# A branch prefetch hint on TensorE ahead of each expert's conditional blocks in the first expert stage

## The chip, the core and the metric

The kernel runs on one core of one Trainium2 chip. The metric is device time in microseconds (us) of one execution, lower is better. Time before: 1584.59 us, the median of 3 runs (1584.36 to 1587.86).

## The reference

Two layers of a diffusion trunk with 256 latent and 256 context tokens of width 1024. Each layer mixes the tokens (conv, pooling, two kinds of attention) and then sends them through a mixture of 16 experts, two experts for each token. Only the mixture matters here:

```python
def expert_block(args):
    xblk, e = args
    a = xblk @ w_gate[e]
    u = xblk @ w_up[e]
    return (jax.nn.silu(a) * u) @ w_down[e]

yb = lax.map(expert_block, (xb, block_exp)).reshape(n_blocks * MOE_BLOCK, d)
y_assign = yb[dest] * sw[:, None].astype(h.dtype)
return jax.ops.segment_sum(y_assign, st, num_segments=t_tok)
```

In the first layer all 512 tokens go through it, so 1024 rows are spread over 16 experts, 64 on average. How many an expert gets is known only when the router has run.

## The kernel before

**The first expert stage** is `moe0`. Experts are taken in order, `e` from 0 to 15. The rows of an expert are cut into chunks of 32. Chunks 0 and 1 are always computed (`gu(e, [0, 1], ...)`: gate and up products, 128 matmuls on TensorE, then `swiglu` on ScalarE and VectorE). A third chunk is computed under `tc.If(v > 64)` and a fourth under `tc.If(v > 96)`, where `v = counts[e]` is the number of rows; inside that, under `tc.If(v > 128)`, there are two loops for still more rows. Each of these extra chunks ends with its own down product (`down_x`, line 1085, 64 matmuls). After the conditional blocks `down(e)` computes the down product of chunks 0 and 1 (line 1076, 32 matmuls) and a scatter on GpSimd writes the rows to `yd` in device memory.

**Control flow.** Each engine has its own instruction stream and its own copy of the conditions in registers. A condition is a COMPARE_AND_BRANCH on each engine; the body of the `If` lies straight behind it and is jumped over when the condition does not hold. The code that is jumped over on TensorE is long: for `v > 64` two gate and up products, two loops with their bodies and two down products; for `v > 96` the same less one of each; for `v > 128` only the two loops. The conditions have the lines 1146, 1148 and 1151 in the profile of before. Line 1127 is a small condition inside `fetch_more`, in which TensorE has no work of its own.

**Order.** The stage stands under `tc.manual_schedule()`, so that each engine takes its instructions in the order in which they are written. For TensorE that is, for one expert: chunks 0 and 1 (line 1023), branch on 64, branch on 96 where it is reached, the extra down products, then `down(e)`, then the next expert.

**Weights.** `Ring` loads 12 pieces of 1 MB for each expert (four pairs of gate and up, four of down) into 11 units of on-chip memory of two pieces each, from the SP queue (`big_load`, line 178), with at most four loads in flight. A load waits until TensorE has read the old content of its place. Ahead of the stage the ring is filled.

**After the stage** the loads of `yd` (line 1180) on the SP queue wait for the last scatter, and loads of `w_mod` for the second layer (line 178) stand behind them on the same queue. The matmuls of line 213 use those.

The lines that the change touches, with their callers:

## Time and profile before

| what | value |
|---|---|
| median of 3 runs | 1584.59 us (1584.36 to 1587.86) |
| the profiled execution, its own time | 1585.9 us |
| its span, first to last instruction | 1584.4 us |
| TensorE matmul busy | 1339.8 us, 85% of the span |
| VectorE busy | 507.2 us, 32% |
| ScalarE busy | 244.5 us, 15% |
| mean rate of all transfers | 324 GB/s |
| waits of TensorE's line 1076 on its own queue at line 1146 | 29.5 us in 8 |
| waits of TensorE's line 1085 on its own queue at line 1148 | 7.6 us in 2 |

Busy shares are means over the whole program. The first expert stage runs from 357.7 to 877.2 us. An engine's queue (PEq or PEldq for TensorE, DVEq for VectorE, SPq for SP) is its sequencer: the branches, waits and transfers that it handles itself are not counted as busy. "PE <- PEq L1146" means that the matmul unit had nothing to do until TensorE's own sequencer was through with the branch of line 1146.

### The profile page before, as it was taken

The numbers are of one execution on the slowest core, as the hardware profiler recorded it, in microseconds if no ns is written. First come the engines' busy times: TensorE is split into PE (matmuls) and PEld (weight loads), VectorE is DVE, ScalarE is ACT, GpSimd is POOL, SyncE is SP. The second block draws the span as 40 slices with busy tenths as digits, with TensorE's granted clock in tenths as the row PEclk, the third lists the DMA queues.
The fourth block names the chain that finished last, engine by engine and source line by source line (L and its number), as shares of the span: only waits on it lengthen the run. The fifth ranks groups of instructions, "written<-read, shape, count | busy, mean of one in ns | idle before, by whom it ended". The sixth has DMA issues, their size and how long they took to land. (4 is left out here: it accounts for less than half of the span.)

```text
span 1584.4 us, 22716 instructions
## 1 busy us (share of the span) xinstructions
PE 1339.8 (85%) x9054; PEld 576.5 (36%) x9054; DVE 507.2 (32%) x1350; ACT 244.5 (15%) x536; POOL 188.0 (12%) x254
## 2 busy tenths in 40 slices
PE   4999999859889887888898299996888898988987
PEld 1754555433222222222332067642332232323333
DVE  2555365671111101111112568743212112112121
ACT  3432143110000000000001265410000000000000
POOL 0411200231111110011110431110000000000000
PEclk9999989979889898999999699997999999999999
DMA  9677875267999999999986753665998899999991
GB/s 362 207 276 266 284 276 200 80 242 279 419 420 420 418 416 419 417 418 418 407 333 195 292 196 121 239 251 212 420 419 356 323 416 419 419 414 420 410 415 40
DMA packets 92349, 513.11 MB, mean 324 GB/s; under 512 B 15872, under 2 KB 19328, under 8 KB 36320
## 3 DMA queue, kind: packets, MB, share of 16 engines
q1 hardware_dynamic: 84320, 490.47, 77.7%
q0 software_dynamic: 6096, 18.42, 3.1%
q8 instruction: 138, 2.26, 0.6%
q10 hardware_dynamic: 1712, 1.27, 0.3%
q14 instruction: 83, 0.68, 0.1%
HBM read 501.80 MB, written 8.32 MB: 322 GB/s over the span
## 5 line engine op out<-in xcount | busy, mean ns | idle before, releaser
L1023 PE MATMUL psg<-u,W 128*32 128x512 f32 x4608 | 531.5, 612 | 68.2 <-DMA u<-in_w_up_dram 15.0
L1023 PEld LDWEIGHTS psg<-u,W 128*32 128x32 f32 x4608 | 159.0, 112 | 428.1 <-issue 364.5
L1076 PE MATMUL pd<-u,W 128*64 128x512 f32 x512 | 135.6, 683 | 39.2 <-PEq L1146 29.5
L1030 DVE TENSOR_TENSOR W<-W,psg 128x256 f32<-128x256 f32 x72 | 30.3, 421 | 381.2 <-ACT W L1029 339.9
L1061 DVE STREAM_TRANSPOSE W<-W 128x256 f32<-128x256 f32 x49 | 30.0, 635 | 324.6 <-DMA W<-h2d,W 297.3
L1232 PE MATMUL pd<-u,x 128*64 128x512 f32 x544 | 120.5, 594 | 15.3 <-DVE x L1031 10.4
L1029 ACT ACTIVATE W<-psg 128x256 f32<-128x256 f32 x72 | 27.6, 383 | 586.8 <-PE psg L1023 567.0
L1076 PEld LDWEIGHTS pd<-u,W 128*64 128x64 f32 x512 | 43.1, 156 | 129.3 <-issue 119.9
L756 PE MATMUL ps<-u,u 128*128 128x512 f32 x192 | 90.1, 614 | 0.0
L213 PE MATMUL psm<-u,W 128*32 128x512 f32 x320 | 47.2, 669 | 35.1 <-DMA u<-in_w_mod_dram 21.7
L1232 PEld LDWEIGHTS pd<-u,x 128*64 128x64 f32 x544 | 44.9, 137 | 84.2 <-issue 78.9
L1053 POOL DMA_INDIRECT W<-h2d,W x49 | 46.9, 956 | 153.5 <-DVE W L1061 132.1
L1057 POOL DMA_INDIRECT yd<-W x23 | 22.9, 996 | 284.0 <-ACT W L1064 261.1
L328 DVE TENSOR_TENSOR x<-u,x 128x512 fp32r<-128x512 f32 (+2 forms) x64 | 42.0, 660 | 42.0 <-ACT x L327 37.6
L1085 PE MATMUL pd<-u,W 128*32 128x256 f32 x448 | 35.5, 462 | 22.5 <-PEq L1148 7.6
L756 PEld LDWEIGHTS ps<-u,u 128*128 128x128 f32 x192 | 35.6, 195 | 43.2 <-issue 42.9
L327 ACT CAST x<-u 128x512 fp32r<-128x512 f32 (+2 forms) x64 | 35.4, 562 | 98.2 <-PE ps L402 46.8
L1234 DVE SCALAR_TENSOR_TENSOR W<-pd,W,x 128x512 f32<-128x512 f32 x17 | 12.8, 751 | 111.2 <-PE pd L1232 111.2
L403 PE MATMUL ps<-u,x 128*128 128x512 f32 (+1 forms) x128 | 44.9, 351 | 1.1 <-DVE x L328 1.0
L401 PE MATMUL ps<-u,x 128*128 128x512 f32 (+1 forms) x128 | 45.2, 353 | 0.0
L1064 ACT COPY W<-pd 128x512 f32<-128x512 f32 (+1 forms) x23 | 12.0, 520 | 212.8 <-PE pd L1076 154.0
L402 PE MATMUL ps<-u,x 128*128 128x512 f32 (+1 forms) x128 | 44.3, 346 | 0.0
(283 smaller groups left out, 1459.7 us busy)
## 6 DMA issues: line engine op xcount, KB each, us to landing
u<-in_w_gate_dram SPq DMA_DIRECT2D x128, 1024.0 KB
u<-in_w_up_dram SPq DMA_DIRECT2D x128, 1024.0 KB
u<-in_w_down_dram SPq DMA_DIRECT2D x128, 1024.0 KB
u<-in_w_mod_dram SPq DMA_DIRECT2D x40, 1024.0 KB
u<-in_w_in_dram SPq DMA_DIRECT2D x12, 1024.0 KB
x<-in_w_mod_dram SPq DMA_DIRECT2D x8, 1024.0 KB
u<-in_w_out_dram SPq DMA_DIRECT2D x4, 2048.0 KB
u<-m_dram POOLq DMA_DIRECT2D x9, 512.0 KB, 7.2
```

Source lines behind the costliest of these rows:

```text
L213: PE.matmul(ps[32 * g:32 * g + 32, :], sc[:, j, :], t[:, 512 * g:512 * g + 512], start=(j == 0), stop=(j == 7), tile_position=(0, 32 * g))
L327: i = S.copy(h, src)
L328: eng.tensor_tensor(l, src, h.bitcast(F32), op=ALU.subtract)
L401: PE.matmul(ps, xh, yh, start=first, stop=False)
L402: PE.matmul(ps, xh, yl, start=False, stop=False)
L403: PE.matmul(ps, xl, yh, start=False, stop=end)
L756: PE.matmul(ps, CT[:, k, 128 * i:128 * i + 128], wout[hh][:, k, :], start=(k == 0), stop=(k == 7))
L1023: PE.matmul(pss[k][32 * g:32 * g + 32, :], xTs[k][:, j, :], w[:, :, 256 * g:256 * g + 256], start=(j == 0), stop=(j == 7), tile_position=( ...
L1053: G.indirect_dma_start(out=XG[b], out_offset=None, in_=src, in_offset=bass.IndirectOffsetOnAxis(ap=ic, axis=0))
L1076: PE.matmul(pd[64 * h:64 * h + 64, :], HP[:, j, :], w[:, 512 * h:512 * h + 512], start=(j == 0), stop=(j == 7), tile_position=(0, 64 * h))
L1085: PE.matmul(pd[32 * g:32 * g + 32, 0:256], hT[:, j, :], w[:, 256 * g:256 * g + 256], start=(j == 0), stop=(j == 7), tile_position=(0, 32 * g))
L1232: PE.matmul(pd[64 * h:64 * h + 64, :], HT[k][:, j, :], w[:, 512 * h:512 * h + 512], start=(j == 0), stop=(j == 7), tile_position=(0, 64 * h))
```

## The change

At the start of each expert's code a hint names the branch on `v > 64`, and at the start of that branch's body a hint names the branch on `v > 96`. Each hint carries the condition's value in a register, computed by an added register operation. Both are on TensorE only. Two labels tie the hints to their branches.

```diff
                 v = counts[e]
                 if e + 1 < NE:
                     fetch(e + 1)
+                tc.mark_branch_hint_location(f"more{e}", v > 64, engines=[ET.PE])
                 gu(e, [0, 1], [0, 1], [None, None])
-                with tc.If(v > 64):
+                with tc.If(v > 64, label=f"more{e}"):
+                    tc.mark_branch_hint_location(f"most{e}", v > 96, engines=[ET.PE])
                     gu(e, [2], [2], ["o"])
-                    with tc.If(v > 96):
+                    with tc.If(v > 96, label=f"most{e}"):
                         tr(XT[0], XG[3])
                         gu(e, [0], [3], ["mod"])
                         with tc.If(v > 128):
```

In the built program TensorE has 32 register operations and 32 hints more (2 of each for each expert) and the other engines have the same instructions as before. Line numbers behind the change are higher by 1 or 2.

The next fence shows TensorE's stream at the branch on 64 of one expert. Names: `psg` is the accumulator of gate and up, `W` holds the rows, `u_...` are ring units; 1146 became 1147 and 1148 became 1150.

```order
-L1146 COMPARE_AND_BRANCH
+L1147 COMPARE_AND_BRANCH
+L1148 REGISTER_ALU
+L1380 BRANCH_PREFETCH_HINT
 L1023 MATMUL psg<-u_71,W 32x512 x8
 L1023 MATMUL psg<-u_6_1290,W 32x512 x8
 L1023 MATMUL psg<-u_64,W 32x512 x8
 L1023 MATMUL psg<-u_70,W 32x512 x8
-L1148 COMPARE_AND_BRANCH
+L1150 COMPARE_AND_BRANCH
```

The hint for the branch on 96 stands at the start of the body, one chunk's product (64 matmuls in the trace) ahead of its branch.

The next two fences show TensorE's stream from the end of the block on 64 of expert 0 to the start of expert 1, before and after (`pd` is the accumulator of the down product).

```order
L1146 UNCONDITIONAL_BRANCH x2
L1076 MATMUL pd<-u_69,W 64x512 x8
L1076 MATMUL pd<-u_67,W 64x512 x8
L1023 MATMUL psg<-u_5_1289,W 32x512 x5
L1127 COMPARE_AND_BRANCH
L1127 UNCONDITIONAL_BRANCH x2
```

After:

```order
L1147 UNCONDITIONAL_BRANCH x2
L1145 REGISTER_ALU
L1380 BRANCH_PREFETCH_HINT
L1076 MATMUL pd<-u_69,W 64x512 x8
L1076 MATMUL pd<-u_67,W 64x512 x8
L1023 MATMUL psg<-u_5_1289,W 32x512 x5
L1127 COMPARE_AND_BRANCH
L1127 UNCONDITIONAL_BRANCH x2
```

The hint for expert 1 stands ahead of `down(0)`, not behind it, so a whole down product, the small branch of line 1127 and the product of chunks 0 and 1 lie between the hint and its branch.

## Rows read from the trace of the kernel before

**Rows 1.** TensorE in order of time, experts 0 and 1 (start, length, idle before).

```profile
375.12 7.09 PE L1076 MATMUL pd<-u,W 128*64 128x512 f32 x32 [1.67 <-DVEq L1146]
382.14 13.94 PE L1023 MATMUL psg<-u,W 128*32 128x512 f32 x128
399.68 9.95 PE L1076 MATMUL pd<-u,W 128*64 128x512 f32 x32 [3.60 <-PEq L1146]
```

**Rows 2.** Four stretches: busy time of each engine, granted TensorE clock, transfer share, GB/s.

```profile
370.00:375.00 5.00, 3.45 (x35) 1.36 (x24) 2.11 (x4) 0.77 (x2) 0.00 (x0) 1.00 0.02 3
400.00:405.00 5.00, 5.00 (x14) 1.50 (x12) 0.60 (x2) 0.00 (x0) 1.89 (x2) 0.50 1.02 417
790.00:795.00 5.00, 4.31 (x27) 1.14 (x31) 0.63 (x2) 0.00 (x0) 0.00 (x0) 0.66 0.40 169
795.00:800.00 5.00, 4.46 (x44) 1.16 (x36) 0.06 (x1) 0.38 (x1) 0.00 (x0) 1.00 0.01 3
```

**Rows 3.** TensorE's queue at lines 1146, 1148, 1151, 1127: min/median/max ns, first and last start.

```profile
L1146 PEldq COMPARE_BRANCH  x22: 70/306/6524, 370.6 to 860.3; - x22
...
L1148 PEldq COMPARE_BRANCH  x7: 65/5923/6127, 454.9 to 833.3; - x7
...
L1151 PEldq COMPARE_BRANCH  x1: 329/329/329, 796.7 to 796.7; - x1
...
L1127 PEldq COMPARE_BRANCH  x17: 82/229/330, 357.7 to 846.4; - x17
```

**Rows 4.** TensorE's queue at line 1146 in expert 0 (368 to 376 us).

```profile
L1146 PEldq COMPARE_BRANCH  x1: 3843/3843/3843, 370.6 to 370.6; - x1
L1146 PEldq EVENT_SEMAPHORE  x1: 51/51/51, 374.5 to 374.5; - x1
```

**Rows 5.** TensorE's queue at line 1148 in expert 10 (660 to 680 us).

```profile
L1148 PEldq COMPARE_BRANCH  x1: 6037/6037/6037, 672.5 to 672.5; - x1
```

**Rows 6.** TensorE in order of time, experts 10 to 15 and the start of the next layer.

```profile
663.03 12.22 PE L1023 MATMUL psg<-u,W 128*32 128x512 f32 x112 [0.50 <-DMA u<-in_w_up_dram]
679.00 4.67 PE L1085 MATMUL pd<-u,W 128*32 128x256 f32 x56 [3.75 <-PEq L1148]
684.53 0.64 PE L1085 MATMUL pd<-u,W 128*32 128x256 f32 x8 [0.87 <-issue]
...
716.59 5.08 PE L1085 MATMUL pd<-u,W 128*32 128x256 f32 x64 [3.66 <-DMA u<-in_w_gate_dram]
...
753.23 4.04 PE L1085 MATMUL pd<-u,W 128*32 128x256 f32 x37 [3.81 <-PEq L1148]
758.88 1.92 PE L1085 MATMUL pd<-u,W 128*32 128x256 f32 x27 [1.60 <-issue]
...
790.69 8.77 PE L1023 MATMUL psg<-u,W 128*32 128x512 f32 x64 [2.14 <-DVE W L1061]
...
837.89 4.23 PE L1085 MATMUL pd<-u,W 128*32 128x256 f32 x64 [1.89 <-DVEq L1148]
...
867.11 10.05 PE L1076 MATMUL pd<-u,W 128*64 128x512 f32 x32 [4.11 <-PEq L1146]
...
897.11 1.94 PE L213 MATMUL psm<-u,W 128*32 128x512 f32 x8 [16.06 <-DMA u<-in_w_mod_dram]
```

**Rows 7.** The SP queue in order of time: weight loads, and the transfers behind the stage.

```profile
375.50 1.57 SPq L178 DMA_DIRECT2D u<-in_w_gate_dram  x1
...
651.26 0.33 SPq L178 DMA_DIRECT2D u<-in_w_up_dram  x1
...
881.75 2.01 SPq L1180 DMA_DIRECT2D u<-yd  x4
883.87 0.94 SPq L178 DMA_DIRECT2D u<-in_w_mod_dram  x2
```

**Rows 8.** What the SP queue waited for: us in total, times, longest.

```profile
SPq L178 <- PEq L1146: 15.9, 1, 15.9
...
SPq L1180 <- DMA yd<-W: 10.4, 1, 10.4
```

## Prediction

> **What bounds the kernel now.** I read the list of TensorE's waits first, then TensorE in order of time over the first expert stage, its own queue at the branches, the transfer share by stretches, and last the SP queue. The question is in which part of the stage TensorE sets the time and in which the weights do.

> Every expert with at most 64 rows jumps over the block of line 1146, and those with 65 to 96 rows jump over the block of line 1148. The jump is slow on TensorE's queue: up to 6.52 us at line 1146, 5.92 us in the median at line 1148, while a condition that falls through costs 0.07 us and the short jumps of lines 1127 and 1151 cost about 0.23 and 0.33 us [rows 3]. Nothing in these rows waits for data in that time, so I read it as the fetch of the instructions at the far end of the jump. In expert 0, with transfers nearly idle (share 0.02, [rows 2]), it took 3.84 us [rows 4]; in expert 10, beside the weights, 6.04 us [rows 5].

> What TensorE loses is less than that, because its queue runs ahead of its matmuls. Expert 10's product ends at 663.03 + 12.22 = 675.25 us and the branch began at 672.5 us. The next matmul comes 3.75 us after the product's end [rows 5, 6]. Some wait would stay with a free branch: the down product needs the activation and the transpose on ScalarE and VectorE. Where the branch is not last this is 1.67 us (expert 0, [rows 1]) and 1.89 us (expert 14, [rows 6]).

> Two further costs hang on the slow jump. First, the granted clock: after expert 1's wait of 3.60 us the clock was 0.50 in 400 to 405 us, the lower level, and `down` took 9.95 us where expert 0's took 7.09 us [rows 1, 2]. Second, the block of instructions behind the target: expert 10 stops again after 56 of 64 matmuls, until 684.53 us, that is 6.0 us after the branch ended at 672.5 + 6.04 = 678.54 us [rows 5, 6]; expert 12 likewise after 37 of 64.

> Up to 663 us the stage goes by the weights. A share of 1.02 stands in 400 to 405 us [rows 2], and the load issued at 651.26 us is what ended the wait at 663.03 us, 11.8 us later [rows 6, 7]. That is TensorE's last wait for weights. From there to the stage's end TensorE is the bound, and at 795 to 800 us the transfers even stand idle (0.01, [rows 2]), since the ring is full. Behind the stage the loads of `yd` wait for the last scatter [rows 8] and come at 881.75 us; the `w_mod` loads behind them, issued at 883.87 us [rows 7], end TensorE's wait of 16.06 us at 897.11 us [rows 6]. So what expert 15 gains is passed on to the next layer.

> **The change part by part.** It removes nothing but time. It adds 32 register operations and 32 hints on TensorE, of which 16 + 6 pairs run (line 1148 has 7 records, 6 conditions and the jump at the end of expert 13's block, [rows 3], so 6 experts pass the condition on 64). No hint runs in the trace of before: those that it has stand in loops that no expert enters. I bound one added instruction from below by the fall-through, 0.07 us, and from above by the near jump, 0.33 us [rows 3]. The queue is 2.75 us ahead of the matmuls (675.25 - 672.5), so I cost them at nothing; without that cover, the 22 instructions of experts 10 to 15 would be 1.5 to 7 us.

> A hinted jump is then bounded below by the near jump, 0.33 us, and above by what it costs now. I take 0.33 us if the hint works, because that is what a jump takes to code that is already there. Is the lead enough? At line 1150 the hint stands one chunk ahead of its branch, 64 matmuls, 6.97 us (half of 13.94, [rows 1]), against a fetch of 6.04 us. It may even be late: the matmuls are not due before 675.25 + 1.89 = 677.14 us, so a branch that ends at about 676.8 us instead of 672.8 us still costs nothing. At line 1147 the lead is a whole down product and a product of two chunks, 21 us [rows 1]. The block behind the target moves forward with the branch by 5.7 us: in expert 10 to 678.8 us, where it is due at 677.14 + 56/64 of 4.23 = 680.8 us; in expert 12 to 753.2 us, where it is due at 753.23 - 3.81 + 1.89 + 37/64 of 4.23 = 753.8 us. So both second stops go, the latter with little to spare.

> Per expert, wait and down product together, now against expert 14 (1.89 + 4.23 = 6.12 us) or expert 0 (1.67 + 7.09 = 8.76 us), all from [rows 1, 6]:
> - Expert 10: 3.75 + 4.67 + 0.87 + 0.64 = 9.93 us, gain 3.8 us.
> - Expert 11: 3.66 + 5.08 = 8.74 us, gain 2.6 us. The row names a load as the end of this wait, but its length is that of the other jumps.
> - Expert 12: 3.81 + 4.04 + 1.60 + 1.92 = 11.37 us, gain 5.3 us.
> - Experts 13 and 14: none. Expert 13 falls through, and its near jump at 1151 is unhinted and cheap; expert 14's wait is already ended by VectorE.
> - Expert 15: 4.11 + 10.05 = 14.16 us, gain 5.4 us.
> - Expert 0: its matmuls wait for VectorE anyway, but the loads of the ring waited for TensorE's queue behind the branch [rows 8]: semaphore at 374.5 us, first load at 375.50 us [rows 4, 7]. The product ended at 375.12 - 1.67 = 373.45 us, so the loads and all that goes by the weights up to 663 us come 1.0 us sooner.
> - Experts 1 to 9: none. TensorE reaches the weights sooner and waits there.

> The sum is 18.1 us. Against it stands the clock. A wait of 2.14 us in expert 13 was followed by 8.77 us for 64 matmuls instead of 6.97 us, at a granted 0.66 [rows 2, 6]; those of 1.67 and 1.89 us were followed by full speed. The four waits that stay are of the latter size, but close, so I allow for half of one such fall and take 17 us. The profiled execution's 1585.9 us becomes 1568.9 us. Its time is 1.3 us above the median, so on the median I forecast 1567.5 us. If no fall comes, and expert 13's goes too, it is 20 us (1564.6 us); if all four come, 18.1 - 7.2 = 10.9 us (1573.7 us).

> **The rivals.**
> *Only the near hints work.* Between the hint for 64 and its branch stands the taken jump of line 1127; if a jump that is not the hinted one makes the sequencer forget the hint, expert 15 and expert 0 gain nothing and only 3.8 + 2.6 + 5.3 = 11.7 us stay: 1572.9 us. For it speaks the order of the instructions; against it, that line 1127's jump is near (0.23 us) and need not throw out what was fetched.
> *Only the far hints work.* The lead at line 1150 fails by over 4 us, because the fetch starts late behind another: 1.0 + 5.4 = 6.4 us, 1578.2 us. For it speaks that fetch and lead are near each other, against it the 4 us of slack.
> *No hint has any effect.* Then the time is 1584.6 us. No row speaks against it, since no hint runs in this trace.
> *Slower: the hinted block takes the place of the next one.* TensorE's queue then meets a missing block in the middle of the product: 6.04 us of fetch less 2.75 us of lead, 3.3 us of idle time. With five hinted jumps in experts 10 to 15 (10, 11, 12, 14, 15) this is 16.5 us. It is slower only if the hinted block, too, has been thrown out when the branch comes; then nothing is gained and the time is 1601.1 us. If the block is still there, the 17 us pay for it. For it speaks that code seems to be held for a short way only: expert 10 had its target block and yet waited 6.0 us for the one behind it. [...]

> **How the numbers follow.** All hints work: 0.50, at 1567.5 us, own range 1564.6 to 1573.7 us. Only the near ones: 0.15. Only the far ones: 0.12. No effect: 0.14. Slower: 0.09. About 0.3%, 4.8 us, is what a measurement of this kernel tells from no change. Faster by more: 0.50 + 0.15 and most of the far case, which is only 6.4 us, 0.10, in all 0.75. Within it: 0.14 + 0.02 = 0.16. Slower: 0.09. The range holds the first three cases, with 2.6 us below the own range's end for stops of the second layer that shift with the code's position, and up to 1584 us for part of the case without effect.

> **What would show it.** Right: the jumps at lines 1147 and 1150 take about 0.3 us on TensorE's queue; VectorE ends the wait ahead of each down product, at 1.7 to 1.9 us; expert 15's `down` takes 7.1 us; the last wait for weights still ends near 662 us, and 897.11 us becomes about 880 us. The near case shows as slow jumps left at 1147, the far case as slow jumps left at 1150, the displaced block as new stops of 3 us inside line 1023. Wrong would be the sum, with all jumps fast, if the weights take over again in experts 11 to 15 (new waits for loads there), if the lower clock follows waits of 1.9 us too, or if the 17 us vanish between 880 us and the end.

## The result and the profile after

The change makes the kernel faster: 1564.22 us, the median of 4 runs (1557.94 to 1571.56), against 1584.47 us before (4 runs). The ratio is 0.9878, 95% interval 0.9848 to 0.9909. Run again as e5 below it gave 1561.73 us against 1584.90 us, ratio 0.9851 (0.9826 to 0.9877). The forecast was 1567.5 us.

The profiled execution is the slowest of the four (1571.56 us, span 1569.4 us), 14.3 us below the profiled one of before. TensorE's queue at the branches and the hints (min/median/max ns, first and last start):

```profile
L1147 PEldq COMPARE_BRANCH  x22: 70/263/3960, 371.3 to 854.1; - x22
...
L1150 PEldq COMPARE_BRANCH  x7: 68/1443/3174, 447.0 to 827.7; - x7
...
L1380 PEldq BRANCH_PREFETCH_HINT  x22: 30/35/44, 352.9 to 834.8; - x22
...
L1145 PEldq ALU_OP  x16: 37/37/51, 352.8 to 834.7; - x16
```

Against [rows 3] the longest jumps fell from 6.5 and 6.1 us to 4.0 and 3.2 us, and the shortest of line 1147's far jumps take 0.33 us, as long as a near jump. A hint and its register operation take 35 and 37 ns. What TensorE waits for ahead of the down product:

```profile
PE pd L1076 <- DVEq L1147: 17.1, 10, 1.7
```

The numbers are us in total, times and the longest: all ten waits of the experts without a third chunk are now ended by VectorE, at 1.7 us each. Experts 10 to 15 in order of time (start, length, idle before), to be held against [rows 6]:

```profile
662.69 12.22 PE L1023 MATMUL psg<-u,W 128*32 128x512 f32 x112 [1.42 <-DMA u<-in_w_up_dram]
676.79 1.50 PE L1085 MATMUL pd<-u,W 128*32 128x256 f32 x23 [1.88 <-DVEq L1150]
681.09 2.53 PE L1085 MATMUL pd<-u,W 128*32 128x256 f32 x41 [2.80 <-issue]
...
713.26 3.66 PE L1085 MATMUL pd<-u,W 128*32 128x256 f32 x64 [1.88 <-DMA u<-in_w_gate_dram]
...
746.56 0.81 PE L1085 MATMUL pd<-u,W 128*32 128x256 f32 x9 [1.88 <-DMA u<-in_w_gate_dram]
749.21 5.81 PE L1085 MATMUL pd<-u,W 128*32 128x256 f32 x55 [1.84 <-issue]
...
795.36 7.33 PE L1085 MATMUL pd<-u,W 128*32 128x256 f32 x128 [1.68 <-DVEq L1153]
...
832.33 3.66 PE L1085 MATMUL pd<-u,W 128*32 128x256 f32 x64 [1.88 <-DVEq L1150]
...
858.61 7.09 PE L1076 MATMUL pd<-u,W 128*64 128x512 f32 x32 [1.73 <-DVEq L1147]
...
884.65 1.94 PE L213 MATMUL psm<-u,W 128*32 128x512 f32 x8 [14.75 <-DMA u<-in_w_mod_dram]
```

The wait ahead of each extra down product is now 1.88 us (1.68 us in expert 13), and expert 15's `down` runs at full speed. But experts 10 and 12 stop a second time, after 23 and 9 of the 64 matmuls, where before it was after 56 and 37. In expert 10 the queue shows why:

```profile
L1150 PEldq COMPARE_BRANCH  x1: 3142/3142/3142, 672.1 to 672.1; - x1
L1150 PEldq EVENT_SEMAPHORE  x1: 51/51/51, 675.4 to 675.4; - x1
```

The jump still took 3.14 us, to 675.24 us, and the block behind the target came 5.85 us after that, at 681.09 us.

To see where the time went I divide each span into three (us): the first expert stage (from the first matmul of line 1023 to the end of expert 15's `down`), the stretch between the stages, and all from the first matmul of line 1023 in the second stage to the end of the span.

| profiled execution | first stage | between | second stage to the end |
|---|---|---|---|
| before | 519.4 | 214.2 | 493.1 |
| the change | 507.4 | 217.4 | 486.3 |
| e5, the change again | 507.0 | 217.2 | 483.0 |
| e1, hints always say not taken | 520.5 | 217.3 | 486.3 |
| e2, hints always say taken | 501.3 | 217.4 | 485.4 |
| e3, hint for 64 alone | 516.4 | 218.4 | 485.9 |
| e4, hint for 96 alone | 513.8 | 213.4 | 486.2 |
| e6, late experts only | 504.1 | 216.0 | 498.2 |
| e7, early experts only | 523.8 | 217.9 | 486.2 |
| e8, hint for 64 always says taken | 501.9 | 219.0 | 480.0 |
| e9, late experts, code in the same place | 510.5 | 217.3 | 482.8 |
| e10, e8 again | 501.4 | 217.1 | 485.1 |
| e11, e10 with hints in the second stage | 501.6 | 217.0 | 459.5 |
| e12, before with hints in the second stage | 518.0 | 218.1 | 459.0 |

For the change the bounds are these rows (the first stage ends at 858.61 + 7.09 us above):

```profile
358.29 15.87 PE L1023 MATMUL psg<-u,W 128*32 128x512 f32 x128 [6.12 <-DVE W L1061]
...
1083.09 16.85 PE L1023 MATMUL psg<-u,W 128*32 128x512 f32 x128 [7.27 <-PEq L1250]
```

So the span's gain of 15.0 us is 12.0 us in the first stage and 6.8 us in the second, less 3.2 us lost between the stages and 0.6 us by which the first stage began later. Each row is one execution. The first stage repeats well (507.4 and 507.0 us; 501.9 and 501.4 us; 519.4 us before and 518.0 us in e12, whose first stage is that of before). The other two parts don't: in the seven profiles whose code lies as in the change and has no hints in the second stage (the change, e1, e2, e5, e8, e9, e10) the second stage took 480.0 to 486.3 us, and e12 took 218.1 us between the stages, where before took 214.2 us, with the code of before but for one hint at the end.

### The profile page after: what moved, and what is told of

Read it like the earlier page. It is cut to its first block, busy times and chain, and to the rows that moved or that the text cites. A ratio compares the mean times of both kernels' runs of the same rounds, so it can differ in the third digit from the quotient of the medians.

```text
span 1569.4 us, 22760 instructions
## 1 busy us (share of the span) xinstructions
PE 1325.1 (84%) x9054; PEld 579.2 (37%) x9054; DVE 507.4 (32%) x1350; ACT 244.5 (16%) x536; POOL 187.3 (12%) x254
## 5 line engine op out<-in xcount | busy, mean ns | idle before, releaser
L1023 PE MATMUL psg<-u,W 128*32 128x512 f32 x4608 | 538.8, 620 | 94.5 <-DMA u<-in_w_up_dram 36.7
L1023 PEld LDWEIGHTS psg<-u,W 128*32 128x32 f32 x4608 | 163.6, 114 | 457.4 <-issue 401.1
L1076 PE MATMUL pd<-u,W 128*64 128x512 f32 x512 | 114.0, 597 | 17.1 <-DVEq L1147 17.1
L1076 PEld LDWEIGHTS pd<-u,W 128*64 128x64 f32 x512 | 39.9, 138 | 89.1 <-issue 84.5
L1085 PE MATMUL pd<-u,W 128*32 128x256 f32 x448 | 30.4, 418 | 18.8 <-issue 7.8
L695 ACT ACTIVATE u<-ps,u,W 128x512 f32<-128x512 f32 (+1 forms) x48 | 33.9, 707 | 35.3 <-DVE u L693 24.3
```

Of the source, the lines that this page charges most:

```text
L695: S.activation(P, ps[:, 0:NK], AF.Exp, bias=nb, scale=cq[:, qt, pos:pos + 1], accum_out=sm_)
L1023: PE.matmul(pss[k][32 * g:32 * g + 32, :], xTs[k][:, j, :], w[:, :, 256 * g:256 * g + 256], start=(j == 0), stop=(j == 7), tile_position=( ...
L1076: PE.matmul(pd[64 * h:64 * h + 64, :], HP[:, j, :], w[:, 512 * h:512 * h + 512], start=(j == 0), stop=(j == 7), tile_position=(0, 64 * h))
```

## The experiments

The kernel before ran beside them on the same chip; its median was 1584.3 us (for e1 to e4), 1584.9 us (e5 to e8) and 1585.1 us (e9 to e12). All start from the changed kernel unless the text says otherwise.

**The hints say nothing useful (e1).** The instructions and their places are those of the change; the register always holds the value that means that the branch falls through.

```diff
-                tc.mark_branch_hint_location(f"more{e}", v > 64, engines=[ET.PE])
+                tc.mark_branch_hint_location(f"more{e}", counts[NE] > 0, engines=[ET.PE])
...
-                    tc.mark_branch_hint_location(f"most{e}", v > 96, engines=[ET.PE])
+                    tc.mark_branch_hint_location(f"most{e}", counts[NE] > 0, engines=[ET.PE])
```

> The same instructions at the same places, but both hints always say that the branch falls through (the register holds the result of 'the largest count is above 0'). Theory A, the gain is the fetch of the far block ahead of the jump: the gain goes, about 1584 us, the jumps at lines 1147 and 1150 take 5.9 us again. Rival B, the gain is the shift of the code by the added instructions: about 1564 us as with the true hints, whatever the hints say.

Measured: 1581.37 us, ratio 0.9978 (0.9956 to 1.0). Its queue, and expert 15's down product:

```profile
L1147 PEldq COMPARE_BRANCH  x22: 70/463/6581, 366.7 to 859.0; - x22
...
L1150 PEldq COMPARE_BRANCH  x7: 68/5959/6140, 451.0 to 832.4; - x7
...
865.86 8.63 PE L1076 MATMUL pd<-u,W 128*64 128x512 f32 x32 [4.16 <-PEq L1147]
```

The slow jumps are back, and so is the first stage (520.5 us). Theory A holds for the first stage. Rival B is not wholly wrong: the second stage takes 486.3 us here as with the change, 6.8 us less than before, although the hints say nothing of use and stand in the first stage alone. What is left to explain it is the shift of the code, with the reserve that the second stage differs by 6 us between profiles of the same code. By the medians e1 is 2.9 us below the kernel before, and its interval reaches 1.0.

The profile counts what the queues for instructions moved (packets, MB, share of the time of 16 transfer engines). Of these two queues only the one shown changes by more than 3 packets between the runs, and only TensorE's code was changed, so I take its packets as TensorE's blocks of code; 2.26 MB in 138 packets are 16.4 KB each in this program. In order: before, the change, e1 and e2.

```profile
q8 instruction: 138, 2.26, 0.6%
q8 instruction: 123, 2.02, 0.5%
q8 instruction: 134, 2.20, 0.6%
q8 instruction: 119, 1.95, 0.5%
```

So true hints did not add fetches: 15 blocks fewer than before were fetched (e5: 124), with 15 far jumps hinted, and with hints that say nothing of use most of them are back. Which block a hint saves, these rows don't show.

**The hints always say taken (e2).** The same edit with `counts[NE] > 511` in both places.

> Both hints always say that the branch is taken. The jumps that are taken keep their gain; the six experts that pass the condition on 64 and expert 13, which passes that on 96, get a hint for a jump that does not come. Theory A with a cheap wrong hint: about 1564 us, the same as the true hints. Rival C, a hinted block takes the place of the next one: new stops of about 3 us inside line 1023 in experts 3 and 10 to 14, those of 10 to 14 in the time, some 15 to 20 us more: about 1580 us.

Measured: 1561.04 us (1557.18 to 1562.65), ratio 0.9846 (0.9815 to 0.9876). Experts 10 to 12:

```profile
673.39 3.66 PE L1085 MATMUL pd<-u,W 128*32 128x256 f32 x64 [1.87 <-DVEq L1150]
...
706.69 3.66 PE L1085 MATMUL pd<-u,W 128*32 128x256 f32 x64 [1.88 <-DVEq L1150]
...
739.99 3.66 PE L1085 MATMUL pd<-u,W 128*32 128x256 f32 x64 [1.88 <-DVEq L1150]
```

Rival C falls: line 1023 has no new stop in these experts; the only new one is of 1.02 us, in line 1085 of expert 13. Nor are wrong hints merely cheap; with them the second stops of experts 10 and 12 are gone, and the first stage is 6 us shorter than with true ones.

**One hint alone (e3, e4).** Only the hint for 64 stays, or only that for 96.

```diff
-                    tc.mark_branch_hint_location(f"most{e}", v > 96, engines=[ET.PE])
```

```diff
-                tc.mark_branch_hint_location(f"more{e}", v > 64, engines=[ET.PE])
```

> Only the hint for the condition on 64. By the sums on the profile after: expert 15 keeps 5.3 us, and expert 0 about 1 us; experts 10 to 12 and 14 lose 6.1 us: about 1584.5 - 6.4 - 3 (second layer) = 1575 us. If the gain were the shift of the code alone, half of the shift would be there and no such split by expert would be seen.

> Only the hint for the condition on 96. Experts 10 to 12 and 14 keep 6.1 us, expert 15 falls back to a wait of 4.1 us and a slow down product (5.3 us more), expert 0 too: about 1584.5 - 6.1 - 3 = 1575 us. With line 1150's jump late by the same 3.1 us as in the profile after if the lead is what lacks; at 0.33 us if the earlier hint for 64 was in its way.

Measured: 1574.54 us, ratio 0.9929 (0.9902 to 0.9957), and 1570.92 us, ratio 0.9905 (0.9873 to 0.9938). Each alone gives a part, 9.8 and 13.4 us. That these add up to about what the change gives says little: in the first stage the parts are 3.0 and 5.6 us, against 12.0 us with both hints, and each profile has the shorter second stage besides (485.9 and 486.2 us), as e1 has. In the second of them expert 15 is back at its slow jump, and line 1150's jump (1149 there) is on the whole no better for the missing hint for 64: it took 0.45 us in expert 10, but 3.5 us in expert 12 and 5.3 us in expert 11:

```profile
860.98 10.82 PE L1076 MATMUL pd<-u,W 128*64 128x512 f32 x32 [3.83 <-PEq L1146]
...
L1149 PEldq COMPARE_BRANCH  x7: 67/1853/5337, 455.5 to 827.7; - x7
```

**The change again, and its halves by expert (e5, e6, e7).** e5 is the change itself; e6 has both hints only from expert 10 on, e7 only up to expert 9.

```diff
-                tc.mark_branch_hint_location(f"more{e}", v > 64, engines=[ET.PE])
+                if e >= 10:
+                    tc.mark_branch_hint_location(f"more{e}", v > 64, engines=[ET.PE])
...
-                    tc.mark_branch_hint_location(f"most{e}", v > 96, engines=[ET.PE])
+                    if e >= 10:
+                        tc.mark_branch_hint_location(f"most{e}", v > 96, engines=[ET.PE])
```

> The change as it is, to compare with the next three on the same chip: about 1564 us (15 to 22 us below the kernel before), with the second stops in experts 10 and 12 at the same matmuls as in its first profile (after 23 and after 9 of 64), since the code lies in the same place.

> Both hints in experts 10 to 15 only. Theory A, up to 663 us the stage goes by the weights: all of the gain but expert 0's 1 us stays, 1564 to 1568 us. With no added instructions ahead of expert 10 the blocks lie nearly as in the kernel before, so the second stops should fall after some 56 and 37 of 64 matmuls in experts 10 and 12 and no longer cost. Rival D, every avoided slow jump counts: nine of the fifteen far jumps that line 1147 and 1150 take lie in experts 1 to 9, so more than half of the gain would go: about 1574 us.

> Both hints in experts 0 to 9 only. Theory A: their jumps become fast, TensorE waits for weights instead, and only expert 0's earlier release of the ring is left: 1 us, about 1583 us. Rival D: more than half of the gain, about 1574 us.

Measured: 1561.73 us for the change; 1576.61 us, ratio 0.9940 (0.9918 to 0.9962) with the late experts only; 1580.89 us, ratio 0.9975 (0.9955 to 0.9994) with the early ones only. The second stops of the change are after 23 and 9 matmuls again, as they are in e1, where the jumps are slow: their place goes with the code and not with the jumps. With the late hints the first stage is shorter than with all of them (504.1 us), since experts 10 and 12 have no second stop; there the jumps of experts 10 to 12 took 0.44 to 0.48 us. Expert 14 has a stop instead, behind a jump of 3.4 us:

```profile
673.27 3.66 PE L1085 MATMUL pd<-u,W 128*32 128x256 f32 x64 [1.88 <-DVEq L1152]
...
820.76 1.50 PE L1085 MATMUL pd<-u,W 128*32 128x256 f32 x23 [1.88 <-DVEq L1152]
824.30 3.84 PE L1085 MATMUL pd<-u,W 128*32 128x256 f32 x41 [2.04 <-issue]
```

The whole, however, is 9 us above the range of Theory A, and by the times alone rival D would have it. The table shows another place: the second stage took 498.2 us. The early half is near what Theory A says in the whole, with the few us that e1 has too. Its first stage is not: expert 10's down product starts 1.1 us sooner than before, as forecast, but the stage is 4.4 us longer. There the second stops of experts 10 and 14 come after 25 and 5 matmuls and take 2.57 and 1.89 us, with slower matmuls behind them.

**The late half with the code in the same place (e9).** All hints stand, but those of experts 0 to 9 always say that the branch falls through.

```diff
+                tc.mark_branch_hint_location(f"more{e}", (v if e >= 10 else counts[NE]) > (64 if e >= 10 else 0), engines=[ET.PE])
...
+                    tc.mark_branch_hint_location(f"most{e}", (v if e >= 10 else counts[NE]) > (96 if e >= 10 else 0), engines=[ET.PE])
```

> The change with its code at the same places, but in experts 0 to 9 both hints always say that the branch falls through; in 10 to 15 they say what is true. In the run with hints in experts 10 to 15 alone the first stage was short (504.1 us against 507.4 with the change), but the second expert stage took 498.2 us against 486.3. Theory G, that was the place of the second stage's code, not the missing hints: with the places as in the change the second stage is back near 486 us and the time is within 2 us of the change, 1562 to 1566 us. Rival D, the hints of experts 1 to 9 carry part of the gain: 1570 us or more.

Measured: 1567.57 us (1562.44 to 1570.32), ratio 0.9879 (0.9849 to 0.9909). Theory G is right on the second stage, 482.8 us. The time is above the bound that I gave for it, though, and below rival D's. Set beside e5, the first stage is 3.5 us longer. Of that 0.6 us is there when expert 10's extra down product starts; nearly all of the rest is slower matmuls, which I put down to the clock. In expert 13 64 matmuls of line 1023 behind the same wait of 2.14 us took 8.77 us in e9 and 7.07 us in e5; with the change they took 8.77 us at a granted 0.80. In expert 12 55 matmuls behind the second stop took 6.08 us, against 4.66 us in e5 (first row e9, second e5); with the change it was 5.81 us at a granted 0.54. Over the whole span the granted clock was 0.935 in e9 and 0.945 in e5:

```profile
748.34 6.08 PE L1085 MATMUL pd<-u,W 128*32 128x256 f32 x55 [1.85 <-issue]
```

```profile
747.65 4.66 PE L1085 MATMUL pd<-u,W 128*32 128x256 f32 x55 [1.82 <-issue]
```

The intervals of the two overlap, so whether the early hints are worth 1 us or a few is not settled.

**Only the hint for 64 always says taken (e8, e10).** This is the edit of e2 in the first place alone; the hint for 96 goes by its value.

> The hint for the condition on 64 always says taken, that on 96 goes by its value. In the run with both always taken, experts 10 and 12 had no second stop. Theory E: the hint for 64 fetched the block of the down product, which lies just behind the target of the jump at line 1150, and it was still there: no second stops in experts 10 to 12 here either, about 1561 us, some 3 us below the change. Rival F, the second stops go because of the hint on 96 in expert 13 or by chance of the run: stops after 23 and 9 of 64 are back, about 1564 us.

> The kernel whose hint for 64 always says taken, once more, as the base of the next run: 1556 to 1560 us, first stage about 502 us, no second stops in experts 10 to 12.

Measured: 1558.31 us, ratio 0.9837 (0.9812 to 0.9862), and 1560.78 us, ratio 0.9831 (0.9801 to 0.9861). e10 is 0.8 us above the range that was expected. The second stops in experts 10 and 12 are gone in both profiles; these are e8's jumps of line 1150, of which the longest is expert 10's, and the products of experts 10 and 12:

```profile
L1150 PEldq COMPARE_BRANCH  x7: 73/354/3532, 439.5 to 814.5; - x7
...
669.39 3.66 PE L1085 MATMUL pd<-u,W 128*32 128x256 f32 x64 [1.87 <-DVEq L1150]
...
735.98 3.66 PE L1085 MATMUL pd<-u,W 128*32 128x256 f32 x64 [1.88 <-DVEq L1150]
```

That is Theory E: the block which the hint for 64 named in vain was of use one jump later. Expert 10's jump was as late here as with the change (3.53 and 3.14 us; 3.87 us in e2), so it is not an earlier jump that took the stop away. Expert 13, which falls through twice, got a new stop of 1.09 us ahead of line 1085's fifth matmul in e8, the one visible cost of a hint for a jump that does not come.

**Hints in the second expert stage too (e11, e12).** Every expert there jumps over a long block at line 1250. The hint for the next expert's branch is set ahead of this expert's matmuls. e11 has this on top of e10, e12 on top of the kernel before.

```diff
-            with tc.If(v > 64 * pair):
+            with tc.If(v > 64 * pair, label=f"pair{cur[0]}" if pair == 1 else None):
...
+        tc.mark_branch_hint_location("pair0", counts[0] > 64, engines=[ET.PE])
...
+                if e + 1 < NE:
+                    tc.mark_branch_hint_location(f"pair{e + 1}", counts[e + 1] > 64, engines=[ET.PE])
                 gu(e, 0, [0, 1], (lambda: combine(OHT[0], [Yh, Yl])) if e else None)
```

> As the run before it, with a hint for the condition of the second expert stage as well, one expert ahead of its branch (its jump takes 6.1 us in the median in every expert). If the weights bound the second stage (transfer share 1.01 in it), TensorE's waits on that branch, 10 to 28 us in the runs so far, turn into waits for weights and only the last expert's wait of 2 us and its slower clock go: 3 to 6 us less, about 1553 us. If TensorE bounds it: 15 to 25 us less, about 1537 us.

> The kernel before, with hints in the second expert stage only. The first stage stays at 519 to 520 us. If the second stage's length (493.1 us before, 486.3 with hints that do nothing, 498.2 in the run with late hints) comes from stops at its jumps and behind them, it falls to 480 us or less: about 1572 us. If it comes from something else that moves with the code, it stays at 485 to 495 us: 1577 to 1585 us.

Measured: 1534.50 us, ratio 0.9679 (0.9650 to 0.9708), and 1551.85 us, ratio 0.9782 (0.9749 to 0.9816). e11 is 26.3 us below e10: the weights as the bound of the stage (3 to 6 us less) are refuted, and the gain is a little above the 15 to 25 us of the other case. e12 is 20 us below its expected 1572 us, since its second stage fell by 34.1 us and not by 13. First e10, then e11: the jumps, one expert's first product, and the transfers at the end of the stage (busy time of each engine, clock, transfer share, GB/s):

```profile
L1250 PEldq COMPARE_BRANCH  x18: 82/6114/6517, 1064.1 to 1512.8; - x18
...
1287.07 8.77 PE L1023 MATMUL psg<-u,W 128*32 128x512 f32 x64 [2.18 <-PEq L1250]
...
1510.00:1520.00 10.00, 7.61 (x40) 2.92 (x44) 2.25 (x5) 0.62 (x1) 0.00 (x0) 1.00 0.83 343
1520.00:1530.00 10.00, 10.00 (x80) 3.55 (x76) 0.00 (x0) 0.00 (x0) 0.00 (x0) 0.83 0.02 7
...
1549.13 1.46 PE L1246 MATMUL acc<-x,x 64*128 64x512 f32 x8
```

```profile
L1250 PEldq COMPARE_BRANCH  x18: 89/365/6204, 1065.0 to 1489.2; - x18
...
1280.69 7.07 PE L1023 MATMUL psg<-u,W 128*32 128x512 f32 x64 [0.60 <-PEq L1250]
...
1510.00:1515.00 5.00, 4.90 (x44) 2.51 (x36) 1.88 (x4) 0.77 (x2) 0.00 (x0) 1.00 0.94 393
1515.00:1520.00 5.00, 4.66 (x22) 1.95 (x24) 0.47 (x2) 0.00 (x0) 0.00 (x0) 1.00 0.29 121
...
1523.98 1.46 PE L1246 MATMUL acc<-x,x 64*128 64x512 f32 x8
```

The jumps fall from 6.1 to 0.37 us in the median, the wait behind most of them from about 2.1 to 0.6 us, and the slower clock behind some of them goes (8.77 us for 64 matmuls, with a granted 0.83 in 1520 to 1530 us of e10, against 7.07 us, with a granted 1.00 in 1250 to 1300 us of e11). TensorE's idle time in that stage that the profile puts down to nothing else (`issue`) falls from 7.6 us in 6 stops to 1.8 us in 2. The loads of the weights end at about the same time in both, some 1516 to 1518 us, as I estimate from these shares. What differs is how far TensorE is behind them: its last matmuls start at 1549.13 us in the one and at 1523.98 us in the other. The ring lets the loads run ahead of TensorE by what it holds, so a full share up to there said nothing about what bounds the stage's end. e12 shows the same with the first stage left as it was. In both, the second stage takes 459 us, with the code in two different places.

## Why the prediction was right, point by point

**The place and the mechanism were right.** The time came from the fetch of the far block: with hints that say nothing of use the jumps take 5.9 us again and the first stage loses its gain (e1), and with true ones 15 blocks fewer are fetched. Expert 15's wait fell from 4.11 to 1.73 us and its `down` from 10.05 to 7.09 us, a gain of 5.3 us where 5.4 was forecast. Expert 11 gained 3.2 us (1.88 + 3.66 us now) where 2.6 was forecast. Expert 0's earlier release of the ring shows as the last wait for weights, which ended 304.4 us after the stage's start instead of 305.3 us: 0.9 us where 1.0 was forecast. The jump of line 1127 between hint and branch does not undo the hint (expert 15's jump took 0.34 us behind one of 0.25 us at line 1127), and each of the two hints carries a part of the gain (3.0 and 5.6 us of the first stage in e3 and e4). The start at 897.11 us moved to 884.65 us, where about 880 us was named.

**The step that failed: "So both second stops go".** Expert 10 took 1.88 + 1.50 + 2.80 + 2.53 = 8.71 us, a gain of 1.2 us instead of 3.8; expert 12 took 1.88 + 0.81 + 1.84 + 5.81 = 10.34 us, 1.0 us instead of 5.3. Three things went wrong in it. I took the position of the stop, 56 and 37 matmuls into the product, from the trace of before, but the added instructions move the code against the blocks, and it is now at 23 and 9 (in e1 too). And I let the block behind the target come 5.7 us sooner, with a jump of 0.33 us; the jump took 3.14 us in expert 10 and 1.44 us in expert 12, and the block comes some 5.9 us after the jump's end in both. With a jump of 0.33 us and the new places, I estimate from these rows that the block would have come at 672.1 + 0.33 + 5.85 = 678.3 us, where it was due at 676.79 + 23/64 of 3.66 = 678.1 us, in expert 10, and at 748.1 us instead of 747.1 us in expert 12: so the late jump makes nearly all of the one stop, and the earlier place about 1 us of the other. Third, expert 14's 4.23 us, which the sums take as the full speed of this product, hid a short second stop: its weight loads have a gap of 0.43 us there, and the same 64 matmuls take 3.66 us at the same granted clock of 1.00 in the profile after. So expert 14 gained 0.6 us where none was forecast, and expert 11 more than forecast. That a jump that is late by 3 us costs nothing by itself was right: the wait ahead of the product is 1.88 us all the same. e6 shows the step as I had meant it, with the jumps of experts 10 to 12 in time and their code nearly where it was: neither stops. The terms of experts 0, 10, 11, 12 and 15 sum to 11.6 us; with 0.6 us in expert 14 and 0.2 us lost in expert 13 that is the 12.0 us of the first stage, against 18.1 us in my sum.

**What made up for it was luck.** The forecast put its whole gain of 17 us into the first stage, which gave 12.0 us. The second stage took 6.8 us less in the profile, and hints without use give the same there (e1), so it is not what the hints say; the shift of the code is the likely cause, but of before there is one profile only, and the change itself took 486.3 and 483.0 us. The stretch between the stages took 3.2 us more, in e1 too; but e12 took 3.9 us more with the code of before up to there, and e4 0.8 us less with shifted code, so this need not be the change's doing. That the forecast of the whole, 1567.5 us, is near the measured time is therefore partly luck: these two fill part of the gap. The profiled execution is besides the slowest of its four, 7.3 us above their median, so the stages account for 15.0 us of a gain of 20.3 us by the medians. I had put the second stage down as a small uncertainty of 2.6 us below.

**The rivals.** That no hint has an effect, or only the near or the far ones, is refuted by e1, e3 and e4 and by the profile after. The rival on the other side, a hinted block that takes the place of the next one, is refuted by e2: seven wrong hints, no such stop in experts 10 to 14 of line 1023, and a first stage 6 us shorter. What spoke for it in the trace of before was the wait for the block behind expert 10's target, 6.0 us; that a hinted block must push out the next one was my assumption, and no run showed it. A block hinted in vain was of use one jump later: with that hint the down products of experts 10 and 12 run through in 3.66 us (e2, e8), where with true hints they stop for 2.80 and 1.84 us.

**The clock.** No slower clock follows the four waits of 1.7 to 1.9 us ahead of the down products of experts 10, 11, 12 and 15: the granted clock is 1.00 in each of these products. It does follow the second stop of 1.84 us in expert 12 (0.54 from 749.2 to 755.0 us), but not the longer one of 2.80 us in expert 10 (1.00 from 681.1 to 683.5 us); in e5 slower matmuls follow both (41 took 3.89 us in expert 10, where they took 2.53 us with the change; 55 took 4.66 us in expert 12, where all 64 take 3.66 us without a stop). What decides whether it follows is not shown.

**Still open.** The hint ahead of line 1150 ran about 6.6 us before its branch, and expert 10's branch ended 9.7 us after it, although the unhinted jump takes 6.0 us. The lead alone does not explain it: in e6 the same hint ahead of the same matmuls was in time (0.44 us). Whether the fetch stood behind another is not shown. Some jumps of line 1147 still took 3.3 to 4.0 us with a lead of some 20 us, all in experts that had waited for weights; nothing waited for them. Nor is it shown which stops make the second stage longer or shorter with the position of the code; only that most of them go when its jumps are hinted.

## What to carry to other kernels

## What the runs showed that was not expected

- A hint takes 35 ns (median of 22), half of the lower bound that I had set for it.
- A hint for a jump that did not come saved the stops one jump later (e2, e8, e10): no second stops in experts 10 to 12, 6 us less in the first stage. I read it as its block having stayed.
- Hints that tell the truth lower the number of code blocks that are fetched: 138 before, 123 with the change, 122 in e12. With hints that always say taken it is 119 (e2, e8, e10), and 105 with the second stage's besides (e11).
- A transfer share of 1.01 stood over most of the second stage with and without its hints, and the stage took 485.1 us in the one case and 459.5 us in the other.
- The kernel with hints in both stages beats both kernels: 1534.50 us, ratio 0.9679 (0.9650 to 0.9708) to the kernel before.
